# Evictions for both token blocks in one instruction, and a fourth pair by seven products in every other chunk of gate and up

## Chip, cores and metric

The kernel runs on one core of a Trainium2 chip. The metric is the device time of one execution in microseconds, as the median of several runs.

## What is computed

One layer of a streaming encoder on 256 tokens of width 2048, in f32. Two SwiGLU feed-forward blocks of width 5632 stand around a mixing stage (latent attention and gated linear attention) and a cross attention to 256 memory tokens. The change concerns the feed-forward blocks:

```python
def swiglu(h, w_gate, w_up, w_down):
    return (jax.nn.silu(h @ w_gate) * (h @ w_up)) @ w_down

x = x + 0.5 * swiglu(rmsnorm(x, ffn1_norm[l]), ffn1_w_gate[l], ffn1_w_up[l], ffn1_w_down[l])
...  # attention, gated linear attention, cross attention
x = x + 0.5 * swiglu(rmsnorm(x, ffn2_norm[l]), ffn2_w_gate[l], ffn2_w_up[l], ffn2_w_down[l])
```

## The kernel before

Tokens stand in two blocks (b = 0, 1) of 128. Every f32 product is made of three matmuls: each operand is split into a high part (rounded to the matmul's own type) and a low part, and high by high, high by low and low by high are added in PSUM. For weights, `parts` (L123) makes the high part with a cast on ScalarE (L128) and the low part with a subtraction on VectorE (L129), for every weight that is loaded.

A feed-forward block (`ffn`, L558) runs over eleven chunks of 512 columns of gate and up, in groups of four, four and three. After each group the down product of that group runs in two passes (n = 0, 2), each over 1024 columns. Each such stage is one call of `pair_gemm` (L223). It runs over units: one unit is a pair of 128-row slices of the contraction with 512 columns of gate and 512 of up (in the down pass, two blocks of 512 columns).

A unit is either plain or mixed. A plain unit is 2 slices by 2 token blocks by 2 column blocks by 3 parts, 24 matmuls. A mixed unit forms the same 2 by 2 by 2 block product by seven products in place of eight (a Strassen-Winograd scheme): 21 matmuls. It pays with sums: `mixed_parts` (L203) adds the raw weights into `wsum` in three VectorE instructions (L208, L213, L214) and splits seven forms in two goes, 1536 and 2048 columns wide, where a plain unit splits 2048 columns once. The activations of a mixed pair stand as seven sums too, made by `split_pair` (L367 to L380) through the scratch tile `f`, of which there is one.

In a gate and up chunk from the third on, the order of the pairs is 1, 0, 3, 2, 5, 4, 6, 7, and pairs 1, 3 and 5 are mixed (`ORDER8`, `MIXED8`, L52). Four of the seven products are summed over the mixed pairs in four PSUM banks of their own (`extra`), and `middle` (L297) combines them into four tiles after the last mixed unit, with one copy on ScalarE and four additions on VectorE. The other products and the plain ones go into four accumulators `acc`, one bank for each token block and column block.

After the last unit the chunk is evicted (L580 to L586): for each token block one subtraction, one Silu on ScalarE, one addition, and one product that also applies the factor of the row norm, 512 columns each. The result is transposed and split a stage later, by pieces in `self.pending` that `pair_gemm` takes up at its steps (L244), which stand after the last mixed unit, or at the end (L293).

Buffers: four for the split weights (`wspl`; a mixed unit takes two, a plain one one), three for raw weights, one for `wsum`. The gemms of the mixing stage (`gemm`, L132) use the same `acc` banks and evict them block by block. Loads of weights are issued by SyncE. The order on each engine's queue is drawn up when the program is built, from the order of the text and from what is ready.

## Time and profile before

| | us |
|---|---|
| median of 3 runs | 1876.89 |
| lowest, highest | 1876.79, 1877.93 |
| the profiled execution | 1876.87 |
| its span, first to last instruction | 1875.1 |
| TensorE (PE) busy | 1856.3 |
| VectorE (DVE) busy | 1556.9 |
| ScalarE (ACT) busy | 1016.0 |
| GpSimd (POOL) busy | 63.5 |

The granted clock of TensorE is 1.0 of full speed throughout. The first FFN runs from about 10 to 718 us, the mixing stage and the cross attention to about 1171, the second FFN to 1871. Recorded matmuls overlap, so their cost is read from start to start. A row of the timeline gives the start in us, the length in us, the engine, the line, the operation, what it writes and reads with shapes, and in brackets the idle time of the engine before it with what ended it.

### The profile page before, as it was taken

What the parts mean: (1) busy time and instruction counts of PE and PEld (TensorE: products, weight loads), DVE (VectorE), ACT (ScalarE), POOL (GpSimd) and SP (SyncE); (2) the same over time, 40 slices, a digit from 0 to 9 for tenths busy, and PEclk for the clock granted to TensorE, in tenths of its full rate; (3) what the DMA queues carried; (4) which work ended last, traced back from release to release, by engine and by line L of the source; (5) the groups of instructions that cost most, each with busy time, mean ns of one, the idle gap of its engine ahead of it and who ended that gap; (6) DMA issues with size and microseconds to landing.
All of it is one profiled execution on the core that took longest, in us unless ns stands there. A gap on an engine that the chain in (4) does not pass through costs nothing.

```text
span 1875.1 us, 21806 instructions
## 1 busy us (share of the span) xinstructions
PE 1856.3 (99%) x8418; PEld 1525.4 (81%) x8418; DVE 1556.9 (83%) x1691; ACT 1016.0 (54%) x1088; POOL 63.5 (3%) x114
## 2 busy tenths in 40 slices
PE   7999999999999999999999999999999999999999
PEld 6788888888888888788778888788888888888887
DVE  7999999889999996555565655999998899999897
ACT  6555454555445554665555665655544555445552
POOL 1000000000000100120100020000000000000000
PEclk9999999999999999999999999999999999999999
DMA  7566566655665545544435554656556665556653
GB/s 247 182 224 202 180 205 214 198 196 201 205 207 192 203 176 181 169 159 146 133 129 210 179 179 135 202 180 218 206 199 207 202 202 187 195 202 205 200 201 135
DMA packets 148072, 356.01 MB, mean 190 GB/s; under 512 B 11018, under 2 KB 11120, under 8 KB 147968
## 3 DMA queue, kind: packets, MB, share of 16 engines
q1 hardware_dynamic: 147360, 354.07, 56.4%
q8 instruction: 66, 1.08, 0.2%
q0 software_dynamic: 608, 0.55, 0.2%
q14 instruction: 38, 0.31, 0.0%
HBM read 352.48 MB, written 2.10 MB: 189 GB/s over the span
## 4 chain that ended last, share of the span: by engine, by line
PE 95%; ACT 2%; DVE 1%; issue 1%; DMA 0%; POOL 0%; SPq 0%; ACTq 0%
PE acc L241 57%; PE acc L142 19%; PE bank L241 14%; PE bank L350 2%; ACT wh L128 1%; ACT junk L384 1%; DVE wl L129 1%; PE bank L950 0%; PE bank L805 0%; PE bank L786 0%; DMA raw<-in_ffn_w_up_dram 0%; PE bank L949 0%; PE bank L1004 0%; PE bank L1013 0%; ACT hth L359 0%
## 5 line engine op out<-in xcount | busy, mean ns | idle before, releaser
L129 DVE TENSOR_TENSOR wl<-raw,wh 128x2048 fp32r<-128x2048 f32 (+4 forms) x405 | 716.6, 1771 | 177.0 <-ACT wh L128 175.8
L128 ACT CAST wh<-raw 128x2048 fp32r<-128x2048 f32 (+4 forms) x405 | 601.7, 1494 | 380.4 <-PE acc L241 146.9
L241 PE MATMUL acc<-wh,hth 128*128 128x512 f32 x1078 | 418.6, 393 | 5.3 <-ACT wh L128 3.6
L241 PE MATMUL acc<-wl,hth 128*128 128x512 f32 x1078 | 418.3, 390 | 1.4 <-DVE wl L129 1.4
L241 PE MATMUL acc<-wh,htl 128*128 128x512 f32 x1078 | 362.8, 390 | 0.0
L128 ACT CAST wh<-wsum 128x2048 fp32r<-128x2048 f32 x98 | 187.6, 1914 | 282.4 <-DVE wsum L214 223.5
L129 DVE TENSOR_TENSOR wl<-wsum,wh 128x2048 fp32r<-128x2048 f32 x98 | 224.5, 2291 | 38.0 <-ACT wh L128 37.9
L241 PEld LDWEIGHTS acc<-wh,hth 128*128 128x128 f32 x1078 | 202.8, 188 | 47.5 <-ACT wh L128 4.3
L241 PEld LDWEIGHTS acc<-wl,hth 128*128 128x128 f32 x1078 | 202.7, 188 | 43.5 <-DVE wl L129 2.4
L241 PEld LDWEIGHTS acc<-wh,htl 128*128 128x128 f32 x1078 | 202.7, 188 | 42.7
L241 PE MATMUL acc<-wh,actph 128*128 128x512 f32 x448 | 175.9, 393 | 0.0
L241 PE MATMUL acc<-wl,actph 128*128 128x512 f32 x448 | 174.4, 389 | 0.0
L241 PE MATMUL acc<-wh,actpl 128*128 128x512 f32 x448 | 145.6, 389 | 0.0
L208 DVE TENSOR_TENSOR wsum<-raw 128x1024 f32<-128x1024 f32 x98 | 119.5, 1220 | 3.6 <-DMA raw<-in_ffn_w_down_dram 1.5
L142 PE MATMUL acc<-wh,hth 128*128 128x512 f32 (+1 forms) x288 | 113.2, 395 | 0.0
L142 PE MATMUL acc<-wl,hth 128*128 128x512 f32 (+1 forms) x288 | 109.9, 383 | 0.0
L241 PE MATMUL bank<-wl,hth 128*128 128x512 f32 x264 | 103.6, 392 | 1.4 <-DVE wl L129 1.4
L241 PE MATMUL bank<-wh,htl 128*128 128x512 f32 x264 | 102.8, 389 | 0.0
L241 PE MATMUL bank<-wh,hth 128*128 128x512 f32 x264 | 98.6, 390 | 0.0
L241 PEld LDWEIGHTS acc<-wh,actpl 128*128 128x128 f32 x448 | 84.0, 188 | 17.9
L241 PEld LDWEIGHTS acc<-wh,actph 128*128 128x128 f32 x448 | 84.1, 188 | 17.0
L241 PEld LDWEIGHTS acc<-wl,actph 128*128 128x128 f32 x448 | 84.2, 188 | 16.9
(280 smaller groups left out, 2395.7 us busy)
## 6 DMA issues: line engine op xcount, KB each, us to landing
raw<-in_ffn_w_down_dram SPq DMA_DIRECT2D x88, 1024.0 KB, 5.0
raw<-in_ffn_w_gate_dram SPq DMA_DIRECT2D x175, 512.0 KB, 3.8
raw<-in_ffn_w_up_dram SPq DMA_DIRECT2D x175, 512.0 KB, 4.7
raw<-in_w_in_dram SPq DMA_DIRECT2D x24, 1024.0 KB, 5.1
raw<-in_w_out_dram SPq DMA_DIRECT2D x16, 1024.0 KB, 5.1
raw<-in_w_in_dram SPq DMA_DIRECT2D x8, 832.0 KB, 4.5
raw<-in_mem_w_k_dram SPq DMA_DIRECT2D x4, 1024.0 KB, 5.1
raw<-in_mem_w_q_dram SPq DMA_DIRECT2D x4, 1024.0 KB, 5.1
```

The lines of the kernel that those rows point to most:

```text
L128: self.last_act = nc.scalar.copy(out=wh, in_=src)
L129: self.last_dve = nc.vector.tensor_tensor(out=wl, in0=src, in1=wh.bitcast(F32), op=ALU.subtract)
L142: self.last_pe = nc.tensor.matmul(out=out[b][c][:, :w], lhsT=high, rhs=part[:, o:o + w], start=start, stop=stop)
L208: nc.vector.tensor_tensor(out=t[:, :2 * CW].rearrange("p (j n) -> p j n", j=2), in0=raw[:, CW:3 * CW].rearrange("p (j n) -> p j n", j=2), ...
L241: self.last_pe = nc.tensor.matmul(out=bank, lhsT=high, rhs=part, start=key not in seen, stop=stop)
L350: nc.tensor.transpose(out=t[:, i * P:(i + 1) * P], in_=src(b, k), identity=self.ident)
L384: self.nc.scalar.activation(out=junk[:, :width], in_=src, func=AF.Square, accum_out=out)
```

## The change

Accumulators become tiles of two banks, one for each column block, that hold both token blocks side by side, in `pair_gemm` and in `gemm`. With them the eviction of a gate and up chunk is one subtraction and one addition of 1024 columns, and one product of 1024 columns. The factor of the row norm is no longer applied by that product but by a second ScalarE pass after each Silu. In the down passes the additions into `xs` also take both token blocks at once, except for the last column block of the whole FFN.

Chunks 3, 5, 7 and 9 of gate and up take pair 4 as a fourth mixed pair and run in the order 1, 0, 3, 2, 5, 6, 4, 7. Since pair 4 is plain in the other chunks, its normalised input has a kind of its own, "both", with eight 128-column slots, of which four serve as the plain form. To make room in SBUF, the mask and `g_out` move from the constants into the work pool of the mixing stage (and their memsets and load to its head), the work tile `t` has five buffers in place of six, and the scratch of GpSimd's DMAs is halved.

```diff
+MIXED_ODD, ORDER_ODD = (1, 3, 4, 5), (1, 0, 3, 2, 5, 6, 4, 7)
+KINDS = {1: "mixed", 3: "mixed", 4: "both", 5: "mixed"}
...
-        self.acc = pool("acc", 4, space=bass.MemoryType.PSUM)
+        self.acc = pool("acc", 2, space=bass.MemoryType.PSUM)
...
+    def accumulators(self, n):
+        accs = [self.acc.tile([P, NB * CW], F32, name="acc") for _ in range(n)]
+        return [[acc[:, b * CW:(b + 1) * CW] for acc in accs] for b in range(NB)] + [accs]
...
-        out = [[self.acc.tile([P, CW], F32, name="acc") for _ in chunks] for _ in range(NB)]
+        out = self.accumulators(len(chunks))
...
+    PLAIN = {
+        "plain": {(0, 0): 0, (0, 1): 1, (1, 0): 2, (1, 1): 3},
+        "both": {(0, 0): 2, (0, 1): 7, (1, 0): 3, (1, 1): 1},
+    }
...
-        out = [[self.acc.tile([P, CW], F32, name="acc") for _ in range(2)] for _ in range(NB)]
+        out = self.accumulators(2)
...
-        mixed = [i for i, (p, _) in enumerate(units) if xs[p][0]]
+        mixed = [i for i, (p, _) in enumerate(units) if p in mixed]
...
-            x = lambda t, k, b: t[:, (2 * k + b) * P:(2 * k + b + 1) * P]
+            x = lambda t, k, b: t[:, self.PLAIN[kind][k, b] * P:(self.PLAIN[kind][k, b] + 1) * P]
...
-        p1, u3 = (self.sums.tile([P, CW], F32, name="su", bufs=4) for _ in range(2))
-        u4, v = (self.sums.tile([P, CW], F32, name="sg", bufs=2) for _ in range(2))
+        up, gate = (self.sums.tile([P, NB * CW], F32, name=name, bufs=n) for name, n in (("su", 2), ("sg", 1)))
+        p1, u3 = up[:, :CW], up[:, CW:]
+        u4, v = gate[:, :CW], gate[:, CW:]
...
-        nc.vector.tensor_tensor(out=s5, in0=a22, in1=a21, op=ALU.subtract)
+        nc.vector.tensor_tensor(
+            out=blocks(4), in0=blocks(1), in1=a21.unsqueeze(1).broadcast_to([P, 2, P]), op=ALU.subtract
+        )
         nc.vector.scalar_tensor_tensor(out=s6, in0=s5, scalar=-1.0, in1=a11, op0=ALU.mult, op1=ALU.subtract)
         nc.vector.tensor_tensor(out=s3, in0=s6, in1=a12, op=ALU.add)
-        nc.vector.tensor_tensor(out=a21, in0=a11, in1=a21, op=ALU.subtract)
...
+        if kind == "both":
+            at = slice(7 * P, 8 * P)
+            nc.scalar.activation(out=th[:, at], in_=t[:, :P], func=AF.Copy, scale=gain(0))
+            nc.vector.scalar_tensor_tensor(
+                out=tl[:, at], in0=t[:, :P], scalar=gain(0), in1=th[:, at].bitcast(F32), op0=ALU.mult, op1=ALU.subtract
+            )
...
-                        ht, [(wg, c * CW), (wu, c * CW)], 0,
-                        ORDER8 if c > 1 else ORDER_NEXT if c else ORDER_LOAD if ahead else ORDER_TURN,
+                        ht, MIXED_ODD if c % 2 and c > 1 else MIXED8, [(wg, c * CW), (wu, c * CW)], 0,
+                        ORDER_ODD if c > 1 and c % 2 else ORDER8 if c > 1 else ORDER_NEXT if c else ORDER_LOAD if ahead else ORDER_TURN,
...
-                    for b in range(NB):
-                        tt(out=sg[b], in0=out[b][0], in1=sg[b], op=ALU.subtract)
-                        nc.scalar.activation(out=sg[b], in_=sg[b], func=AF.Silu, scale=rstd()[:, b:b + 1])
-                    for b in range(NB):
-                        tt(out=a[b], in0=out[b][1], in1=a[b], op=ALU.add)
-                    for b in range(NB):
-                        stt(out=a[b], in0=a[b], scalar=rstd()[:, b:b + 1], in1=sg[b], op0=ALU.mult, op1=ALU.mult)
+                    tt(out=sg, in0=out[NB][0], in1=sg, op=ALU.subtract)
+                    for b, g in enumerate(halves(sg)):
+                        nc.scalar.activation(out=g, in_=g, func=AF.Silu, scale=rstd()[:, b:b + 1])
+                        nc.scalar.activation(out=g, in_=g, func=AF.Copy, scale=rstd()[:, b:b + 1])
+                    tt(out=a, in0=out[NB][1], in1=a, op=ALU.add)
+                    tt(out=a, in0=a, in1=sg, op=ALU.mult)
...
+                        up, gate = self.middle(extra)
+                        for c, t, f in ((1, up, 0.5), (0, gate, -0.5)):
+                            stt(out=xc[c], in0=both(t), scalar=f, in1=xc[c], op0=ALU.mult, op1=ALU.add)
...
+            self.mask = self.work.tile([P, 2 * P], F32, name="mask", bufs=1)
+            nc.gpsimd.memset(self.mask, 0.0)
+            nc.gpsimd.memset(self.mask[0:64, P + 64:2 * P], NEG)
+            self.g_out = self.work.tile([P, GV], F32, name="g_out", bufs=1)
+            nc.gpsimd.dma_start(out=self.g_out, in_=io["gla_out_norm"][0:1, :].broadcast_to([P, GV]))
...
-            zq = self.work.tile([P, CW], F32, name="t", bufs=6)
+            zq = self.work.tile([P, CW], F32, name="t", bufs=5)
...
-    nc = bacc.Bacc("TRN2", target_bir_lowering=False, num_devices=1, dynamic_dma_scratch_size=4096)
+    nc = bacc.Bacc("TRN2", target_bir_lowering=False, num_devices=1, dynamic_dma_scratch_size=2048)
```

## Rows read from the trace of the kernel before

**Rows 1.** The page, part 1: busy time, share of the span, instructions of each engine.

```profile
PE 1856.3 (99%) x8418; PEld 1525.4 (81%) x8418; DVE 1556.9 (83%) x1691; ACT 1016.0 (54%) x1088; POOL 63.5 (3%) x114
```

**Rows 2.** Timeline of chunk 3, first FFN: first matmuls of three successive units.

```profile
156.85 0.39 PE L241 MATMUL bank<-wh,hth 128*128 128x512 f32 x1
...
161.61 0.39 PE L241 MATMUL acc<-wh,hth 128*128 128x512 f32 x1
...
167.05 0.39 PE L241 MATMUL bank<-wh,hth 128*128 128x512 f32 x1
```

**Rows 3.** Busy time by stretch, chunks 1, 9, 10: length, then each engine (instructions).

```profile
61.45:104.21 42.76, 42.76 (x191) 34.98 (x192) 41.78 (x40) 25.33 (x20) 0.00 (x0) 1.00 0.59 190
...
567.19:609.62 42.43, 42.43 (x192) 35.14 (x191) 38.11 (x36) 23.83 (x18) 0.00 (x0) 1.00 0.61 199
609.62:652.06 42.44, 42.44 (x193) 35.13 (x191) 38.87 (x43) 22.56 (x16) 4.92 (x10) 1.00 0.59 199
```

**Rows 4.** Timeline of DVE from chunk 9 into chunk 10.

```profile
577.19 1.22 DVE L208 TENSOR_TENSOR wsum<-raw 128x1024 f32<-128x1024 f32 x1
...
579.78 1.75 DVE L129 TENSOR_TENSOR wl<-raw,wh 128x1536 fp32r<-128x1536 f32 x1
582.98 2.29 DVE L129 TENSOR_TENSOR wl<-wsum,wh 128x2048 fp32r<-128x2048 f32 x1 [1.45 <-ACT wh L128]
585.19 2.29 DVE L129 TENSOR_TENSOR wl<-raw,wh 128x2048 fp32r<-128x2048 f32 x1
...
603.00 2.28 DVE L129 TENSOR_TENSOR wl<-wsum,wh 128x2048 fp32r<-128x2048 f32 x1
...
609.91 1.28 DVE L584 TENSOR_TENSOR su<-acc,su 128x512 f32<-128x512 f32 x2
611.11 1.41 DVE L586 SCALAR_TENSOR_TENSOR su<-su,sm,sg 128x512 f32<-128x512 f32 x2
612.43 0.69 DVE L213 TENSOR_TENSOR wsum<-wsum,raw 128x512 f32<-128x512 f32 x1
```

**Rows 5.** Timeline of PE at the start of chunk 10: first extra, first accumulator.

```profile
609.62 0.39 PE L241 MATMUL bank<-wh,hth 128*128 128x512 f32 x1
...
612.35 0.39 PE L241 MATMUL acc<-wh,hth 128*128 128x512 f32 x1
```

**Rows 6.** Timeline of PE in the fourth unit of chunk 1: first and last matmul.

```profile
78.22 0.39 PE L241 MATMUL bank<-wh,hth 128*128 128x512 f32 x1
...
82.75 0.39 PE L241 MATMUL bank<-wh,htl 128*128 128x512 f32 x1
```

**Rows 7.** Timeline of DVE for that unit: its second low part.

```profile
78.98 2.29 DVE L129 TENSOR_TENSOR wl<-wsum,wh 128x2048 fp32r<-128x2048 f32 x1 [0.37 <-ACT wh L128]
```

**Rows 8.** Groups by line and form: count, busy us and mean ns, idle before.

```profile
L362 DVE SCALAR_TENSOR_TENSOR htl<-bank,gains,hth 128x256 fp32r<-128x256 f32 x52 | 23.8, 479 | 11.9 <-ACT hth L359 11.5
...
L380 DVE TENSOR_TENSOR htl<-f,hth 128x896 fp32r<-128x896 f32 x6 | 6.5, 1086 | 0.3 <-ACT hth L379 0.2
...
L375 DVE TENSOR_TENSOR f<-f 128x128 f32<-128x128 f32 x22 | 6.3, 284 | 0.6 <-ACT f L373 0.6
```

**Rows 9.** Timeline of PE where chunk 1 of the first FFN begins.

```profile
61.45 0.47 PE L241 MATMUL acc<-wh,hth 128*128 128x512 f32 x1 [1.67 <-DVE sg L581]
```

**Rows 10.** Timeline of DVE in chunk 0: end of one mixed split.

```profile
29.52 1.09 DVE L380 TENSOR_TENSOR htl<-f,hth 128x896 fp32r<-128x896 f32 x1 [0.25 <-ACT hth L379]
```

**Rows 11.** Timeline of ACT in chunk 0: beginning of the same split.

```profile
25.52 0.82 ACT L373 ACTIVATE f<-bank,gains 128x256 f32<-128x256 f32 x2
```

**Rows 12.** Timeline of PE where the second gemm of the mixing stage begins.

```profile
756.80 0.39 PE L142 MATMUL acc<-wh,hth 128*128 128x512 f32 x1
...
757.26 0.40 PE L142 MATMUL acc<-wh,hth 128*128 128x512 f32 x1
```

**Rows 13.** Timeline of DVE there: eviction of the second block.

```profile
757.00 0.51 DVE L699 COPY t<-acc 128x336 f32<-128x336 f32 x1 [1.08 <-PE acc L142]
```

**Rows 14.** Timeline of POOL at the end of the first FFN: the b_gate load.

```profile
705.78 0.59 POOL L679 DMA_DIRECT2D b_gate<-in_gla_b_gate_dram  x1 [49.03 <-DVE htl L362]
```

More of the change, by code (lines that the diff above doesn't have):

```diff
@@ L221, in mixed_parts, with pair_gemm @@
         return forms
-    def pair_gemm(self, xs, cols, k0, order, middle, ahead=None):
+    def pair_gemm(self, xs, mixed, cols, k0, order, middle, ahead=None):
         nc = self.nc
-        out = [[self.acc.tile([P, CW], F32, name="acc") for _ in range(2)] for _ in range(NB)]
+        out = self.accumulators(2)
         if ahead:
@@ L251, in pair_gemm @@
             last = u == len(units) - 1
-            is_mixed, xh, xl = xs[p]
+            is_mixed = u in mixed
+            kind, xh, xl = xs[p]
             with ExitStack() as first:
@@ L307, in middle @@
         add(u4, extra["p5"], u4)
-        return p1, u4, u3, v
+        return up, gate
     def later(self):
@@ L345, in split_pair @@
         nc = self.nc
-        mixed, th, tl = dst
+        kind, th, tl = dst
+        mixed = kind != "plain"
         t = self.bank()
@@ L384, in sum_sq, with new_ht @@
         self.nc.scalar.activation(out=junk[:, :width], in_=src, func=AF.Square, accum_out=out)
-    def new_ht(self, mixed=()):
-        pairs = []
+    def new_ht(self, kinds={}):
+        pairs, width = [], {"plain": 4 * P, "mixed": 7 * P, "both": 8 * P}
         for p in range(KD // 2):
-            width = (7 if p in MIXED8 else 4) * P
-            tiles = [self.keep.tile([P, width], F32R, name=f"ht{h}{p}") for h in "hl"]
-            pairs.append((p in mixed, *(t if p in mixed else t[:, :4 * P] for t in tiles)))
+            tiles = [self.keep.tile([P, width[KINDS.get(p, "plain")]], F32R, name=f"ht{h}{p}") for h in "hl"]
+            kind = kinds.get(p, "plain")
+            pairs.append((kind, *(t[:, :width[kind]] for t in tiles)))
         return pairs
@@ L477, in setup_mix @@
         bc = lambda ap, n: ap.broadcast_to([P, n])
-        self.g_out = const.tile([P, GV], F32, name="g_out")
-        nc.gpsimd.dma_start(out=self.g_out, in_=bc(io["gla_out_norm"][0:1, :], GV))
         freq = room[:, 0:32]
@@ L667, in mix_and_cross @@
             with left("mem") as mem:
-                mt = [(False, *(mem.tile([P, 4 * P], F32R, name=f"mt{h}{p}") for h in "hl")) for p in range(KD // 2)]
+                mt = [("plain", *(mem.tile([P, 4 * P], F32R, name=f"mt{h}{p}") for h in "hl")) for p in range(KD // 2)]
                 mss = self.sm([P, NB, NCH])
@@ L763, in gla_qk @@
         for b in range(NB):
-            gq = self.work.tile([P, CW], F32, name="t", bufs=6)
+            gq = self.work.tile([P, CW], F32, name="t", bufs=5)
             nc.scalar.activation(out=gq, in_=out[b][0], func=AF.Copy, scale=r1k[:, b:b + 1])
@@ L823, in gla_gate @@
             for c in range(2):
-                gate = self.work.tile([P, CW], F32, name="t", bufs=6)
+                gate = self.work.tile([P, CW], F32, name="t", bufs=5)
                 nc.scalar.activation(out=gate, in_=out[b][c], func=AF.Silu, scale=r1[:, b:b + 1])
@@ L1044, in raw @@
             for b in range(NB):
-                row = self.work.tile([P, CW], F32, name="t", bufs=6)
+                row = self.work.tile([P, CW], F32, name="t", bufs=5)
                 (nc.vector.tensor_copy if b else nc.scalar.copy)(out=row, in_=out[b][0])
@@ L1117, in run, with stage @@
         io = self.io
-        def stage(g, mixed=()):
+        def stage(g, kinds={}):
             ht, ss, r = [], self.sm([P, NB, NCH]), []
```

46 lines of the change are left out of this document (24 added, 22 removed).

## The prediction

> **What bounds the kernel now.** I read the busy table first, then the matmuls of one chunk in order of time, then the busy time by chunk, then VectorE (DVE) instruction by instruction, because the change puts work on DVE to take work off TensorE (PE). The reader is to see four things.
>
> PE is busy for 1856.3 of 1875.1 us [rows 1], and the matmuls of a chunk start at an even step. A mixed unit of 21 matmuls takes 161.61 - 156.85 = 4.76 us and a plain one of 24 takes 167.05 - 161.61 = 5.44 us, so one 512-column matmul costs 0.2267 us in both [rows 2]. PE sets the end.
>
> DVE is close behind. In chunk 9 of the first FFN it is busy 38.11 of 42.43 us, and in chunk 1, where it is pressed, 41.78 of 42.76 [rows 3]. So a pressed DVE still loses about 0.98 us in a chunk to dependences.
>
> In the settled chunks DVE runs ahead. The last part that the first unit of chunk 10 needs is finished at 603.00 + 2.28 = 605.28 [rows 4] and PE enters that unit at 609.62 [rows 5]: 4.3 us ahead. An idle time of it in chunk 9 (1.45 us before 582.98) ends with ScalarE's (ACT's) cast [rows 4], which itself has to wait for a buffer that PE gives back.
>
> Where DVE is late, PE's order can hide it. In a unit that begins at 78.22 [rows 6] the second half of the low parts lands at 78.98 + 2.29 = 81.27 [rows 7], 3.05 us after the unit has begun; yet its matmuls go on at 0.2265 us (78.22 to 82.75, twenty steps) [rows 6], because a product with another destination was put between.
>
> **The change part by part.** The sum is made against the profiled execution, 1876.87 us with a span of 1875.1; the median of the runs, 1876.89, is the same number.
>
> *Matmuls taken away.* Chunks 3, 5, 7 and 9 of each FFN turn pair 4 from plain (24 matmuls) into mixed (21). Eight pairs by 3 by 0.2267 us is **-5.44 us**, on the path, since PE sets the end. It can't be more; it is less by what follows.
>
> *DVE work added in those chunks.* A mixed unit costs DVE 2.59 us for the three sums (577.19 to 579.78), 1.67 for the first low part (1.75 recorded; starts come 0.08 before the recorded end) and 2.21 for the second (582.98 to 585.19), together 6.47; a plain one costs 2.21 [rows 4]. So +4.26 us. The evictions give some back. Two 512-column ones take 1.20 us (609.91 to 611.11) and the two products 1.32 (611.11 to 612.43) [rows 4]; with the gate's pair, costed like the up's, 3.72. In their place come three instructions of 1024 columns at 1.14 each, from the 1.22 recorded for that width less 0.08 [rows 4]: 3.42, a saving of 0.30. A merged eviction therefore saves little; DVE pays by the column. Chunk 9 then needs 38.11 + 4.26 - 0.30 = 42.07 and 0.98 of gaps, against PE's 42.43 - 0.68 = 41.75: DVE falls back by 1.3 us in an odd chunk. The even chunk after it, chunk 10, has 42.44 - 38.87 = 3.6 us of idle time to recover [rows 3].
>
> *The joint from an odd chunk to the next stage* (eight of them). The mixed pairs now end at the seventh unit and not at the fifth, so the four sums of the middle (4 by 0.60) and the two splits of the waiting activations (0.60, and 1.7 for a mixed one), 4.7 us by the same widths, come together with the evictions. DVE was 4.3 us ahead there [rows 4, 5]; 4.3 - 4.7 - 1.3 makes it about 1.7 us late in the next mixed units. PE hid 3.05 us of such lateness [rows 6, 7], so most of this should be hidden, with 1.3 us to spare. The four PSUM banks of the middle also have only one plain unit (5.44 us) to come free instead of three, and the second split's transposes come after the chunk. None of this is in the trace. Bounds: 0, by [rows 6]; 1.7 us a joint, if nothing is hidden. I take 0.15 a joint, near the row: **+1.2 us**. A gain is excluded, since the joint only gets more work.
>
> *ACT.* The factor of the row norm leaves DVE's product and becomes a second ACT pass over each 512-column half, and the new mixed units add two wide casts for one. ACT is busy 54% [rows 1] and has some 18 us idle in a chunk. The product waits longer for the second half, but what waits for the product is only the split a chunk later. If that cover went, it would cost the two added passes, about 1.4 us in a chunk; I take 0.
>
> *The first chunks.* Pair 4 of the normalised input gets the kind "both" in each FFN: its low parts cost two instructions of 0.40 spacing now (0.48 recorded), and then one of 896 columns (1.00), one of 256 (0.40) and three of 128 (0.20 each) [rows 8]: 2.0 for 0.8, or +1.2. The evictions of this chunk return 0.3. DVE is what PE waits for at the start, as at 61.45 [rows 9], so I put all of it on the path: 0.9 by 2, **+1.8 us**. Bounds: 0, if it falls into a wait for ACT or DMA; and 5.1 us in the first FFN, since the scratch tile f has one buffer, and a mixed split holds it from 25.52 [rows 11] to 29.52 + 1.09 [rows 10]. The row with the stop speaks for DVE's time, not for f, because pair 4 is needed only in the fourth unit.
>
> *Wider accumulators.* A tile now holds both token blocks of a chunk column and is given back when both are evicted. In FFN chunks that begin with a mixed pair this hides: the first product into it comes 2.73 us after the chunk's start (612.35 - 609.62) [rows 5], and the old evictions end at 611.19 [rows 4]. From chunk 0 to chunk 1 it does not: the first unit is plain, PE already waits 1.67 us there in the first FFN [rows 9], and one long instruction releases half an eviction later. I take **+0.4 us** for both FFNs (0 to 1.2).
>
> *Wider accumulators in the middle of the kernel.* The gemms between the FFNs use the same tiles, and some twelve of their joints evict block by block. One of them: the next gemm begins at 756.80 and its second column at 757.26 [rows 12]; the second block of the old column is copied from 757.00 to 757.51 [rows 13]. Before, that column only needed the first block. Now it waits 0.25 us, unless PE's order takes other products first, as in [rows 6]. Bounds 0 and 1.0 us a joint (a wider eviction with one instruction ahead of it). I take 0.05: **+0.6 us**.
>
> *Moves taken at nothing.* The mask's memsets and the load of g_out leave POOL's queue in the setup and go to the head of the mixing stage, ahead of the b_gate load, which is issued at 705.78 [rows 14] and used in the gemm that begins at 756.80 [rows 12]: some 50 us of cover. Five work buffers for six: never more than four are held but in the last head's overlap with the gates. Half the scratch of POOL's DMAs could delay the loads of the setup, a few us once; the trace shows no row for it, and I take 0. The merged additions into x save 0.1 us or so of DVE in the down stages, where it is not what PE waits for.
>
> Sum: -5.44 + 1.2 + 1.8 + 0.4 + 0.6 = -1.44, so 1876.87 - 1.44 = **1875.4 us**.
>
> **A rule weighed.** DVE's next instruction starts 0.08 us before the recorded end of the one before it (the pair at 609.91, recorded 1.28, is followed at 611.11) [rows 4]. The Trainium skill, VectorE: DVE Perf Modes, "The DRAIN you can't avoid", says that the next operation doesn't start until the pipeline is empty. If each of some 36 instructions of a chunk held DVE for its whole recorded time, an odd chunk would need 36 by 0.08 = 2.9 us more, and the joints would be 4.6 us late instead of 1.7, 1.55 beyond what PE's order hid: 8 by 1.55 in place of the 1.2 taken is 1886.6 us. The start-to-start times speak against it, and I give it 0.02.
>
> **The rivals.**
> *The whole saving arrives.* All joints are hidden and the split of pair 4 falls into waits: only 0.8 us or so is lost, 1872.2 us. For it: PE's even step under a late DVE [rows 6]. Against it: the stop at 61.45 [rows 9].
> *DVE becomes the bound at the joints* (slower). The order of the queues no longer hides the 1.7 us, each of the eight joints costs it, and 1875.4 - 1.2 + 13.6 = 1887.8 us. It decides from the point where a joint's lateness passes the 3.05 us that [rows 6, 7] show hidden; the step on which it hangs is the 4.7 us of work put in one place.
> *The accumulators' release* (slower). The twelve joints between the FFNs cost about 0.6 us each instead of 0.05: 1875.4 - 0.6 + 7.2 = 1882.0 us. For it: the time at 757.51 against 757.26. Against it: PE's free order.
> *The change doesn't do what it says*: the merged evictions leave DVE's time as it is, and the chunk lengths don't fall by 0.68 us because other waits fill them: about 1877.
>
> **How the numbers follow.** Forecast 0.50; whole saving 0.22; DVE bound at the joints 0.13; accumulators 0.11; the skill's rule 0.02; no effect 0.02. A measurement of this kernel can tell some 0.2%, or 3.75 us, from no change, so same means 1873.1 to 1880.6. Faster: 0.22. Slower: 0.13 + 0.11 + 0.02 = 0.26. Same: 0.52. The likeliest case has its own range of 1873 to 1880. The range runs from 1871.0 (the saving of 5.44 and some of DVE's at the start) to 1883.0 (the accumulators' case inside, the DVE case left out with the rule's, 0.15).
>
> **What would show it.** Odd chunks of 41.7 to 42 us on PE instead of 42.43, and even ones unchanged at 42.43, would show the saving and the joints right. A gap of PE in the first two units after an odd chunk, released by a low part or by a bank, shows the joint's price. The first chunk of each FFN longer by about 1 us shows pair 4; PE waits for the accumulators at the gemms' joints show that rival. DVE busy about 41.7 in an odd chunk shows the price of the mixed unit. The prediction is wrong if PE's step under a late DVE doesn't stay at 0.2267 us, or if a transfer or a bank that I count as covered turns up as PE's releaser.

## The result: 15.6 us slower

The changed kernel takes 1892.53 us (median of five runs, 1891.73 to 1894.05) against 1876.89 of the kernel before: a ratio of 1.0081, 95% interval 1.007 to 1.0093. The forecast was 1875.4 with a range of 1871.0 to 1883.0, so the time lies 9.5 us above the range. The profiled execution of after has a span of 1890.8 us, 15.7 more than that of before.

Part 1 of the page of after, which answers [rows 1]:

```profile
PE 1860.1 (98%) x8394; PEld 1523.2 (81%) x8394; DVE 1581.3 (84%) x1597; ACT 1049.5 (56%) x1144; POOL 55.5 (3%) x114
```

The 24 matmuls fewer are there (8418 to 8394), yet PE is busy 3.8 us longer (part of that is the granted clock, see the last section) and idle 12 us longer. What it waited for is the next view, the waits of PE in after: engine, tile and line that waited, what released it, then us in total, how often, the longest.

```profile
PE bank L254 <- DVE htl L403: 7.3, 1, 7.3
...
PE bank L1034 <- DVE s L1023: 1.4, 1, 1.4
PE acc L150 <- ACT t L855: 1.4, 1, 1.4
PE acc L254 <- DVE sg L599: 1.3, 2, 1.0
PE bank L1095 <- DVE t L1104: 1.2, 1, 1.2
PE bank L910 <- DVE rope L574: 1.1, 1, 1.1
PE acc L150 <- ACT v L903: 1.0, 1, 1.0
```

L254 is the matmul of the FFN stages, L150 that of the gemms between the FFNs; L910, L1034 and L1095 are the small work beside those gemms. Before had one such wait in the middle, 0.7 us on rope. So the places are the start of the first FFN (7.3 in one stop) and the middle (many of 1 to 1.4). The settled chunks answer [rows 3]; chunks 1, 9 and 10 of after (length, then busy time and instructions of PE, PEld, DVE, ACT, POOL, granted clock, DMA):

```profile
66.94:109.47 42.53, 42.53 (x192) 35.26 (x192) 41.34 (x34) 24.94 (x20) 0.00 (x0) 1.00 0.60 198
571.05:612.66 41.61, 41.61 (x189) 34.48 (x188) 37.65 (x31) 24.23 (x19) 0.00 (x0) 1.00 0.63 203
612.66:655.45 42.79, 42.79 (x194) 35.07 (x193) 41.69 (x43) 26.67 (x24) 4.90 (x10) 1.00 0.58 198
```

PE is without idle time here: the odd chunk fell from 42.43 to 41.61, the next rose from 42.44 to 42.79. That is a gain of 0.47 a pair of chunks, 3.8 us in eight, near the 4.24 (5.44 less 1.2) of the sum. The loss lies elsewhere.

The table has the length of each stretch, from the first product of a stage to that of the next, as the difference to before in us (the last stretch ends where the last product starts). *Moves* has the moved tiles and one thing more of the change, the split of a mixed pair, which makes two of its four 128-column sums in one instruction of 256 columns; all columns to its right and after have both. *Pair* adds the fourth pair without two-bank accumulators, *wide* the reverse, *middle* is the whole change with one-bank accumulators in the gemms; *best* is the run of the fourth pair in chunks 4, 6, 8 (and 10), with late sums. They are told below.

| stretch | before | after | moves | pair | wide | middle | best |
|---|---|---|---|---|---|---|---|
| up to the first product | 10.35 | -1.8 | -2.3 | -2.0 | -2.2 | -2.0 | -2.2 |
| first FFN, chunk 0 | 51.10 | +7.3 | +0.1 | +4.1 | +1.6 | +7.4 | +0.1 |
| first FFN, rest | 657.37 | -2.0 | 0.0 | +1.1 | +2.5 | -1.4 | -2.0 |
| middle (all gemms) | 453.34 | +10.7 | +0.4 | +0.3 | +10.7 | +0.4 | +0.3 |
| second FFN, chunk 0 | 44.73 | +2.6 | -1.2 | -1.2 | +2.1 | +0.3 | -1.2 |
| second FFN, rest | 653.63 | -1.8 | 0.0 | -2.7 | +2.2 | -1.7 | -2.5 |

### The profile page after: what moved, and what is told of

The parts are those of the page before. It is cut to its first block, busy times and chain, and to the rows that moved or that the text cites. A ratio compares the mean times of both kernels' runs of the same rounds, so it can differ in the third digit from the quotient of the medians.

```text
span 1890.8 us, 21665 instructions
## 1 busy us (share of the span) xinstructions
PE 1860.1 (98%) x8394; PEld 1523.2 (81%) x8394; DVE 1581.3 (84%) x1597; ACT 1049.5 (56%) x1144; POOL 55.5 (3%) x114
## 3 DMA queue, kind: packets, MB, share of 16 engines
q8 instruction: 66, 1.08, 0.2%
## 4 chain that ended last, share of the span: by engine, by line
PE 94%; ACT 2%; DVE 1%; issue 1%; DMA 1%; POOL 1%; SPq 0%; DVEq 0%; ACTq 0%
PE acc L254 56%; PE acc L150 18%; PE bank L254 15%; PE bank L366 2%; ACT wh L136 1%; ACT junk L409 1%; DMA raw<-in_ffn_w_up_dram 1%; PE bank L980 0%; PE bank L835 0%; PE bank L816 0%; PE bank L979 0%; PE bank L1034 0%; PE bank L1043 0%; DVE wl L137 0%; POOL sm L97 0%
## 5 line engine op out<-in xcount | busy, mean ns | idle before, releaser
L254 PE MATMUL acc<-wh,hth 128*128 128x512 f32 x1038 | 407.1, 394 | 3.9 <-ACT wh L136 2.6
L254 PE MATMUL acc<-wl,hth 128*128 128x512 f32 x1038 | 406.2, 392 | 0.8 <-DVE wl L137 0.7
L136 ACT CAST wh<-wsum 128x2048 fp32r<-128x2048 f32 x106 | 202.7, 1913 | 276.1 <-DVE wsum L227 226.4
L254 PE MATMUL acc<-wh,htl 128*128 128x512 f32 x1038 | 354.3, 391 | 0.4 <-DVE htl L378 0.4
L137 DVE TENSOR_TENSOR wl<-wsum,wh 128x2048 fp32r<-128x2048 f32 x106 | 242.8, 2291 | 44.0 <-ACT wh L136 43.9
L254 PEld LDWEIGHTS acc<-wh,hth 128*128 128x128 f32 x1038 | 195.8, 189 | 45.7 <-ACT wh L136 3.2
L254 PEld LDWEIGHTS acc<-wl,hth 128*128 128x128 f32 x1038 | 196.1, 189 | 42.0 <-DVE wl L137 2.2
L254 PEld LDWEIGHTS acc<-wh,htl 128*128 128x128 f32 x1038 | 195.6, 189 | 42.2 <-DVE htl L378 1.1
L254 PE MATMUL acc<-wh,actph 128*128 128x512 f32 x448 | 175.8, 393 | 0.0
L254 PE MATMUL acc<-wl,actph 128*128 128x512 f32 x448 | 174.3, 389 | 0.0
L254 PE MATMUL acc<-wh,actpl 128*128 128x512 f32 x448 | 145.8, 389 | 0.0
L221 DVE TENSOR_TENSOR wsum<-raw 128x1024 f32<-128x1024 f32 x106 | 129.2, 1219 | 1.5 <-DMA raw<-in_ffn_w_up_dram 0.9
L254 PE MATMUL bank<-wh,hth 128*128 128x512 f32 x296 | 112.5, 393 | 7.3 <-DVE htl L403 7.3
L254 PE MATMUL bank<-wl,hth 128*128 128x512 f32 x296 | 116.2, 392 | 0.0
L254 PE MATMUL bank<-wh,htl 128*128 128x512 f32 x296 | 115.6, 391 | 0.0
L150 PE MATMUL acc<-wh,hth 128*128 128x512 f32 (+1 forms) x288 | 113.8, 395 | 1.3 <-ACT v L903 1.0
L150 PE MATMUL acc<-wl,hth 128*128 128x512 f32 (+1 forms) x288 | 110.1, 383 | 0.0
L254 PEld LDWEIGHTS acc<-wh,actpl 128*128 128x128 f32 x448 | 84.1, 188 | 17.7
L254 PEld LDWEIGHTS acc<-wl,actph 128*128 128x128 f32 x448 | 84.2, 188 | 17.0
L254 PEld LDWEIGHTS acc<-wh,actph 128*128 128x128 f32 x448 | 84.1, 188 | 17.0
```

The lines of the kernel that those rows point to most:

```text
L136: self.last_act = nc.scalar.copy(out=wh, in_=src)
L137: self.last_dve = nc.vector.tensor_tensor(out=wl, in0=src, in1=wh.bitcast(F32), op=ALU.subtract)
L150: self.last_pe = nc.tensor.matmul(out=out[b][c][:, :w], lhsT=high, rhs=part[:, o:o + w], start=start, stop=stop)
L221: nc.vector.tensor_tensor(out=t[:, :2 * CW].rearrange("p (j n) -> p j n", j=2), in0=raw[:, CW:3 * CW].rearrange("p (j n) -> p j n", j=2), ...
L254: self.last_pe = nc.tensor.matmul(out=bank, lhsT=high, rhs=part, start=key not in seen, stop=stop)
```

## Experiments

### Which half of the change, and which gemms

One-bank accumulators in the gemms alone, the rest of the change kept (the mixing stage opens a pool of four banks, each FFN one of two tiles of two banks):

```diff
-        out = self.accumulators(len(chunks))
+        out = [[self.acc.tile([P, CW], F32, name="acc") for _ in chunks] for _ in range(NB)]
...
+            self.acc_pool(weights, 4)
```

> The changed kernel, but the gemms between the two FFNs have one-bank accumulators again (four of 512 columns, each token block with its own), while gate, up and down keep the two-bank ones. Theory A (the release of the two-bank accumulators makes the 10.8 us that the stretch from the end of the first FFN to the start of the second lost): that stretch returns to within 1 us of the kernel before, and the time to about 1892.5 - 10.8 = 1881.7 us. Theory B (the five work buffers in place of six, or the mask and g_out set up late, make it): the stretch stays 10 us longer, about 1892.5. The first 60 us are unchanged in both: TensorE stops for about 7.3 us at 25.6.

Measured: 1881.18 us, ratio 1.0019 (1.0009 to 1.0028). The middle returns to +0.4, and 2.3 of the 2.6 us at the start of the second FFN go with it; those are time at a lower granted clock (last section). Theory A holds; the five work buffers and the late mask and g_out cost the middle 0.4 us at most.

The change without the fourth pair:

```diff
-MIXED_ODD, ORDER_ODD = (1, 3, 4, 5), (1, 0, 3, 2, 5, 6, 4, 7)
-KINDS = {1: "mixed", 3: "mixed", 4: "both", 5: "mixed"}
+KINDS = {1: "mixed", 3: "mixed", 5: "mixed"}
...
```

> The changed kernel without the fourth mixed pair: no chunk has it and pair 4 is split plainly, everything else of the change stays (two-bank accumulators, merged evictions, moved tiles, five work buffers). Theory A: the 10.8 us of the middle stay, the stop at the start (5.5 us in the first FFN, 2.5 in the second) goes, and the saving of the chunks (3.8 us) goes too: 1876.9 + 10.8 = 1887.7, with 0.4 more at most for the joint of the first chunks. Theory C (the middle is late only because the fourth pair leaves late work of the first FFN to it): about 1877.

Measured: 1894.62 us, ratio 1.0089 (1.0074 to 1.0104), 6.9 us above what Theory A gave. The middle is the +10.7 of after, so Theory C falls. What I had not counted is the FFNs: with the wide evictions and without the fourth pair they are 1.6 + 2.5 + 2.1 + 2.2 us longer than before. Part of it stands in PE's waits of this run, at the down stages, for activations of the last chunk that come late:

```profile
PE acc L253 <- DVE actpl L370: 3.3, 5, 0.9
```

The fourth pair alone (with the moves and the split):

```diff
-        self.acc = pool("acc", 2, space=bass.MemoryType.PSUM)
+        self.acc = pool("acc", 4, space=bass.MemoryType.PSUM)
...
-                    tt(out=sg, in0=out[NB][0], in1=sg, op=ALU.subtract)
...
+                        tt(out=sg[b], in0=out[b][0], in1=sg[b], op=ALU.subtract)
```

> The other half alone: the fourth mixed pair, the kind both and the moved tiles with five work buffers, but the accumulators and evictions of the kernel before (one bank each, block by block). Theory A: the middle is as before, so 1876.9 + 5.5 + 2.5 - 3.8 = 1881.1 us. Theory B: the moves are still in it, so about 1892. The stop of 7.3 us at 25.6 stays in both.

Measured: 1875.72 us, ratio 0.9987 (0.9977 to 0.9996): a small gain where 1881 was expected. The middle is clean again. Two-bank tiles in the FFNs are thus worth 5.5 us of loss (1881.18 - 1875.72). One thing is new here: stage dn8.0 of the first FFN, the first down pass after chunks 8 to 10, is 4.1 us longer.

Whether the instruction or the tile costs those 5.5 us: the run with one-bank gemms, where gate and up evict their shared tiles in 512-column instructions as before.

```diff
-                    tt(out=sg, in0=out[NB][0], in1=sg, op=ALU.subtract)
...
+                        tt(out=s_[b], in0=out[b][0], in1=s_[b], op=ALU.subtract)
+                        nc.scalar.activation(out=s_[b], in_=s_[b], func=AF.Silu, scale=rstd()[:, b:b + 1])
```

> The run with one-bank accumulators in the middle (1881.2 us), where gate and up now evict their two-bank tiles in 512-column instructions, token block by token block, with the row factor in the product, as the kernel before; the tiles are still shared by both blocks. The runs with and without the FFNs' two-bank tiles and merged evictions stand 5.5 us apart (1881.2 and 1875.7): 0.2 us in each of eight joints, 3.4 in the first chunk of the first FFN, 1.5 in that of the second. Theory K (the instruction of 1024 columns and the chain through a second ScalarE pass cost it): nearly all of it returns, about 1876.5. Theory L (the shared tile costs it: what is given back later, or read only when both blocks are written): it stays, 1881.

Measured: 1880.88 us, ratio 1.0015 (1.0006 to 1.0024). Nothing returns, Theory L: it is not the width of the eviction, but what the two blocks share. The stage after a chunk with the fourth pair is 0.30 us longer with halves, 0.34 with wide instructions and 0.13 with one-bank tiles. This run keeps the merged additions into x and the sums' tiles in SBUF, which both blocks share too; that the PSUM tile is what costs was shown for the gemms (below), not for the FFNs.

### How a shared tile costs time in a gemm

DVE and PE where the second gemm begins; first after, which answers [rows 12, 13] (L729 copies out of the accumulators, L736 is a transpose beside the gemm):

```profile
760.42 0.32 PE L150 MATMUL acc<-wh,htl 128*128 128x336 f32 x1
...
760.78 0.92 DVE L729 COPY t<-acc 128x336 f32<-128x336 f32 x2 [2.32 <-PE acc L150]
...
761.34 0.28 PE L736 MATMUL bank<-ident,t 128*16 128x128 f32 x1 [0.60 <-DVE t L729]
761.85 0.47 PE L150 MATMUL acc<-wh,hth 128*128 128x512 f32 x1 [0.23 <-DVE t L729]
```

then the run with one-bank gemms (L735 is the same copy, L154 the same matmul):

```profile
758.55 0.51 DVE L735 COPY t<-acc 128x336 f32<-128x336 f32 x1
...
760.50 0.32 PE L154 MATMUL acc<-wh,htl 128*128 128x336 f32 x1
760.66 0.39 PE L154 MATMUL acc<-wh,hth 128*128 128x512 f32 x1
...
760.86 0.51 DVE L735 COPY t<-acc 128x336 f32<-128x336 f32 x1 [1.08 <-PE acc L154]
```

With one-bank tiles the copy of the first token block runs at 758.55, while PE is still at the second block, and the next gemm follows in 0.16 us. With the shared tile both copies stand after the last product (760.42 + 0.32 = 760.74, copies from 760.78), although the first block was done over 2 us earlier. The next gemm starts 1.43 us after that product. The transposes that the queue puts ahead need the same copy and wait for it too, which is why the waits of the middle bear names like t and rope and not only acc.

If it is that, the order of the products should return it where a gemm has two column blocks:

```diff
-            order = [(c,) for c in range(len(chunks))] if last else [tuple(range(len(chunks)))]
-            turns = [(b, cs, j) for b in range(NB) for cs in order for j in range(nk)]
-            if not last:
+            edge = last or not i
+            order = [(c,) for c in range(len(chunks))] if edge else [tuple(range(len(chunks)))]
+            turns = [(b, cs, j) for cs in order for b in range(NB) for j in range(nk)]
+            if not edge:
```

> The changed kernel with its two-bank accumulators, but the gemms between the FFNs go through their first and last slab of weights by column block and not by token block: all products into the first accumulator tile (both token blocks), then all into the second. Theory F (in the middle the eviction of a two-bank tile starts only after the last product into it, so the first token block's eviction no longer runs under the second one's products): with this order the first tile is complete half a slab before the end again and the next gemm starts on it; the joints of gemms with two column blocks (GQ, k0, GV, k1, ZR, wo0, 8.3 us in sum in the change) fall to under 2 us together, while those of the gemms with one column block, whose only tile can't be complete early (mk to mo0, 3.8 us), stay; the time is about 1892.5 - 6.5 = 1886. Theory G (a two-bank tile costs at any order, by its release or by two engines in its banks at once): the joints stay, about 1892.

Measured: 1887.62 us, ratio 1.0051 (1.0035 to 1.0066), 4.9 below after. The stage that ends at the joint into GV, 1.99 us longer in after than before, is 0.10 longer here; at the joint into ZR 2.38 became 0.72. In sum (net of what next stages give back) the gemms with two column blocks fell from 6.4 to 3.4 us, those with one stayed (3.9 and 4.1). The last gemm, with two column blocks again, gives 1.2 more, and chunk 0 of the second FFN 1.1. Theory F holds in kind; it returned half and not three quarters. PE at that joint, after and then this run:

```profile
828.85 0.27 PE L910 MATMUL bank<-ident,rope 128*128 128x128 f32 x1
830.14 0.50 PE L150 MATMUL acc<-wh,hth 128*128 128x512 f32 x1 [1.02 <-ACT v L903]
```

```profile
828.29 0.27 PE L911 MATMUL bank<-ident,q 128*128 128x128 f32 x1
828.39 0.50 PE L150 MATMUL acc<-wh,hth 128*128 128x512 f32 x1
```

### The start of the first FFN

In after PE stands still from 25.90 to 33.16; the rows of ACT, DVE and PE answer [rows 9 to 11] (L389 copies pair 4's transposes into f, L403 makes the low part of its eighth slot from the bank of the transposes, L399 is the last use of f by the split before, L366 are transposes):

```profile
24.87 1.03 PE L366 MATMUL bank<-ident,xs 128*128 128x128 f32 x8
...
27.52 1.08 DVE L399 TENSOR_TENSOR htl<-f,hth 128x896 fp32r<-128x896 f32 x1
...
28.20 1.89 ACT L136 CAST wh<-wsum 128x2048 fp32r<-128x2048 f32 x1
29.99 0.84 ACT L389 ACTIVATE f<-bank,gains 128x256 f32<-128x256 f32 x2
...
32.67 0.34 DVE L403 SCALAR_TENSOR_TENSOR htl<-bank,gains,hth 128x128 fp32r<-128x128 f32 x1
...
33.16 0.77 PE L254 MATMUL bank<-wh,hth 128*128 128x512 f32 x1 [7.26 <-DVE htl L403]
```

What waits is the first product of a mixed unit, for one of its four banks, which pair 4's split still holds. f, with one buffer, is free of the split before at 27.52 + 1.08 = 28.60, and ACT, which makes a cast until 30.09, copies pair 4 into it only from 29.99. The first run takes the eighth slot from f, so that the bank is free sooner:

```diff
+        if kind == "both":
+            at = slice(7 * P, 8 * P)
+            nc.scalar.copy(out=th[:, at], in_=a21)
+            nc.vector.tensor_tensor(out=tl[:, at], in0=a21, in1=th[:, at].bitcast(F32), op=ALU.subtract)
...
-            nc.scalar.activation(out=th[:, at], in_=t[:, :P], func=AF.Copy, scale=gain(0))
```

> The changed kernel, but the eighth slot of pair 4 (high and low part) is made from the scratch tile f, ahead of the sums that overwrite it, and no longer from the PSUM bank of the transposes, so that this bank comes free when f has been copied, as for the other mixed pairs. Theory D (the stop at 25.6 us is the wait of the first mixed unit for that bank, which the eighth slot's low part gives back last): the stop shortens from 7.3 to the time at which f is copied, about 30.8, so by about 2.2 us, and the time falls by 2 to 3 us, to about 1890; the stop then ends with the copy into f. Theory E (the stop is DVE's load and f's single buffer alone, the bank is no part of it): the stop keeps its 7 us and the time stays at 1892.5.

Measured: 1893.66 us, ratio 1.0081 (1.0066 to 1.0096), no gain. The stop itself is shorter by 2.3 us, as Theory D said, and ends with the copy into f, but other waits follow and chunk 1 begins at 66.94 as in after:

```profile
PE bank L254 <- ACT f L389: 5.0, 1, 5.0
...
PE acc L254 <- DVE wl L137: 1.6, 1, 1.6
...
PE bank L254 <- DVE htl L378: 1.0, 1, 1.0
```

So the bank sets where PE stops, and the work of the fourth mixed split sets when chunk 0 ends. To take that work away, on one-bank accumulators: pair 4 is split plainly, and its sums are made in chunk 2 from its own high and low parts.

```diff
+    def sum_pair(self, dst):
...
+        tt(out=f[:, :4 * P], in0=th[:, :4 * P].bitcast(F32), in1=tl[:, :4 * P].bitcast(F32), op=ALU.add)
...
+                    if c == 1:
+                        self.pending.append(lambda: self.sum_pair(ht[4]))
```

> The fourth mixed pair with the accumulators and evictions of the kernel before (as in the run with that half alone, 1875.7 us), but pair 4 is split plainly at the start, and its four sums are made in the third chunk, from its high and low parts, by five DVE instructions and one ScalarE cast. Theory D (what the start lost, 4.1 us in the length of the first chunk, is the mixed form of pair 4, by f and by the bank): the stop of TensorE at 25 us is gone and the first chunk is as long as before (51.1 us); time about 1875.7 - 4 = 1872 us. Theory H (the start is later by the moved set-up of the constants): the first chunk stays 4 us longer and the time at 1875.7. The stretch dn8.0 of the first FFN (set-up of the mixing stage, 4.1 us longer with the fourth pair alone) is unchanged in both.

Measured: 1873.79 us, ratio 0.9978 (0.9969 to 0.9987). The stop is gone and chunk 0 is 0.8 us longer in place of 4.1 (it begins 2.3 us sooner). Theory D. But the stage after chunk 3 is now 1.03 and 1.30 us longer in the two FFNs, so 1.9 us are left of the expected 4.

### DVE's reserve

Without the fourth pair in chunk 9 of the first FFN:

```diff
+        odd = (3, 5, 7) if ahead else (3, 5, 7, 9)
```

> The same with late sums, and chunk 9 of the first FFN without the fourth pair (chunks 3, 5, 7 there, 3, 5, 7, 9 in the second). Theory I (the 4.1 us of the stretch dn8.0 come from DVE, which has the fourth pair's work of chunk 9 still to make up when the set-up of the mixing stage is put on it): the stretch is as before, at the price of one saving of 0.67, so 3.4 us below the kernel with late sums, about 1868.5. Theory J (an accident of the order, not DVE's load): the stretch stays longer and the time is 0.7 above the kernel with late sums.

Measured: 1872.00 us, ratio 0.9968 (0.9956 to 0.9981). dn8.0 is as long as before (0.01 us more), Theory I: DVE still owed work when the set-up of the mixing stage was put on it. The gain is 1.8 us and not 3.4, since that stage was only 2.4 us longer in the run with late sums; the rest of the 4.1 with the fourth pair alone was the granted clock (last section). The load is not the whole cause: after and the run with one-bank gemms have the fourth pair in chunk 9 too, and dn8.0 is not longer there (+0.01 and +0.03 us). In those two the set-up's work on DVE begins 3.5 us into the stage, in the two runs that lose 1.0. So its place in the queue counts as well, and Theory J is not excluded.

The same seven chunks, moved away from chunk 3:

```diff
-        odd = (3, 5, 7) if ahead else (3, 5, 7, 9)
+        odd = (4, 6, 8) if ahead else (4, 6, 8, 10)
```

> Late sums as before, with the fourth pair in chunks 4, 6, 8 of the first FFN and 4, 6, 8, 10 of the second, so seven as in the run with 3, 5, 7 and 3, 5, 7, 9 (1872.0 us), but never in the chunk right after the one that makes the late sums. In that run the stage after chunk 3 was 1.03 and 1.29 us longer, against 0.13 after the other chunks. Theory O (DVE has not made up the late sums and the start when chunk 3 begins): these 2.1 us go, 1869.9 us. Theory P (the stage after the first chunk with the fourth pair is longer whichever it is): 1872.

Measured: 1869.74 us, ratio 0.9957 (0.9944 to 0.9969), where 1869.9 was expected. Theory O. This run is faster than the kernel before by 0.43%, and than the change by 1.2%.

And in every chunk of gate and up from 4 on, but 9 and 10 of the first FFN:

```diff
+        odd = (4, 5, 6, 7, 8) if ahead else (4, 5, 6, 7, 8, 9, 10)
```

> The fourth pair in every chunk from the fifth on: 4 to 8 of the first FFN, 4 to 10 of the second, twelve in all. By DVE's need as the prediction worked it out (42.07 us and 0.98 of gaps, so 43.05 in such a chunk against 41.75 of TensorE), DVE falls back 1.3 us in each and has no chunk to recover except the down stages. Theory Q (that sum is right, and DVE's lead of 4.3 us is used up by the second chunk in a row): the third and fourth in a row are longer, 42 to 43 us, and the time is not under that of seven chunks, 1870 to 1874. Theory R (DVE's need is overstated, since TensorE hides late parts): each chunk brings its 0.67, twelve of them 3.4 us more than seven: about 1867.

Measured: 1884.33 us, ratio 1.0033 (1.002 to 1.0047), 10 us above the 1870 to 1874 that were expected. Busy time in chunks 4 to 7 of the first FFN, columns as above:

```profile
271.81:312.61 40.80, 40.80 (x181) 33.78 (x180) 38.16 (x33) 21.91 (x14) 0.00 (x0) 1.00 0.61 206
312.61:354.31 41.70, 41.70 (x190) 34.40 (x188) 40.30 (x36) 23.90 (x19) 0.00 (x0) 1.00 0.60 201
354.31:397.69 43.38, 42.65 (x192) 34.26 (x190) 41.61 (x39) 21.87 (x17) 0.00 (x0) 1.00 0.50 171
397.69:442.71 45.02, 43.03 (x191) 34.24 (x190) 43.66 (x40) 26.56 (x21) 0.00 (x0) 1.00 0.54 187
```

Two chunks in a row are short, the third and fourth are not, with DVE pressed (43.66 of 45.02). Theory Q in kind; the price in the pressed chunk is some 2 us above the 43.05 of the sum.

### The moved set-up

The moves and the split, with nothing else of the change:

```diff
-        nc.gpsimd.dma_start(out=self.g_out, in_=bc(io["gla_out_norm"][0:1, :], GV))
...
+            self.g_out = self.work.tile([P, GV], F32, name="g_out", bufs=1)
+            nc.gpsimd.dma_start(out=self.g_out, in_=io["gla_out_norm"][0:1, :].broadcast_to([P, GV]))
```

> The kernel before with the moved tiles alone (mask and g_out set up at the head of the mixing stage, five work buffers, half the scratch of GpSimd's DMAs), no fourth pair, accumulators and evictions as before. In every run with the moves TensorE's first product starts about 2 us earlier. Theory M (the moves give a gain of their own: two things fewer in the set-up): 1876.9 - 2 = 1875 us, the middle unchanged. Theory N (the 2 us are lost again in the first chunk, which waits for the loads of x and weights anyway): 1877.

Measured: 1873.97 us, ratio 0.9976 (0.9968 to 0.9985), a gain of 3.9 us where the prediction had the moves at nothing. 2.3 us come ahead of the first product, 1.2 in chunk 0 of the second FFN. Since the split is in it, this run does not show the moves by themselves.

The load of g_out moved by its line alone:

```diff
-        nc.gpsimd.dma_start(out=self.g_out, in_=bc(io["gla_out_norm"][0:1, :], GV))
...
+            nc.gpsimd.dma_start(out=self.g_out, in_=io["gla_out_norm"][0:1, :].broadcast_to([P, GV]))
```

> The kernel before with one line moved: the load of g_out (128 KB, one row broadcast to 128 partitions) is issued at the head of the mixing stage and not in the set-up. Its tile, the mask, the six work buffers and the scratch stay as they were. Theory S (that load takes the DMA engines from x and the first weights in the first 10 us; the trace of the kernel before has them move as little as 89 GB/s around 6 us, and without it 253 to 307 there): the first product starts 2 us earlier, as with all the moves, and the time is 1876.9 - 2.2 = 1874.7, or 1874 if the 1.2 us of the second FFN's first chunk belong to it too. Theory T (the scratch, the mask's memsets or the five buffers): 1877.

Measured: 1877.96 us, ratio 0.9999 (0.999 to 1.0008). It told nothing, since the load did not move: its tile was free, so it was put into POOL's queue at the old place (row one). The first cast of weights waits as before (row two):

```profile
1.85 0.78 POOL L634 DMA_DIRECT2D g_out<-in_gla_out_norm_dram  x1
...
9.05 1.04 ACT L128 CAST wh<-raw 128x1024 fp32r<-128x1024 f32 x1 [1.56 <-DMA raw<-in_ffn_w_up_dram]
```

With the tile in a pool that opens after the first FFN:

```diff
-        self.g_out = const.tile([P, GV], F32, name="g_out")
...
+            self.g_out = self.work.tile([P, GV], F32, name="g_out", bufs=1)
```

> The kernel before, with g_out's tile in the work pool of the mixing stage and its load issued there (the pool opens only after the first FFN, so the load can't be drawn ahead, as it was in the last run); five work buffers for t, since the tile needs the room. Mask and scratch as before. Theory S (the load of g_out in the set-up delays the first weights): the first product starts at about 8.1 us in place of 10.35, and the time is 1874 to 1875. Theory T (the halved scratch, or the mask's memsets, make the earlier start): the first product starts at 10.2 again, and 1877.

Measured: 1876.06 us, ratio 0.999 (0.998 to 0.9999). The first product starts at 8.19, Theory S, and the cast waits for no load:

```profile
7.11 1.04 ACT L128 CAST wh<-raw 128x1024 fp32r<-128x1024 f32 x1
```

Of the 2.2 us, 0.75 are lost in chunk 0 and 0.73 in dn8.0; the span is 0.5 us below that of before, the median 1.9 below the 1877.96 that before measured beside it. So this load explains the earlier start, and at most half of the 3.9. What the rest is (mask, scratch, the split, or the queue order that comes with them) stays open. For the 1.2 us in the second FFN the split is the nearest candidate, though it was not run by itself: chunk 0 there, where DVE splits pair after pair, is 44.73 us before, 44.76 and 44.73 in the last two runs, which have the old split, and 43.51 to 43.55 in the six runs with the new split, all the moves and one-bank tiles everywhere.

## Why the prediction was wrong, point by point

- **Matmuls right, joints near.** -5.44 + 1.2 was forecast for the eight pairs of chunks, -3.8 measured. Of the 0.68 that three matmuls are worth, the chunk and the stage after it keep 0.47 with shared tiles, so a joint costs 0.21, 1.7 us in eight. With one-bank tiles they keep 0.65 (-0.78, then +0.13), so the joint itself costs 0.03. The 0.15 taken lies between the two; that the total came near is in part luck, since the 0.2 belongs to the shared tiles and not to the work that was counted.
- **DVE's need: right in kind.** The odd chunk's surplus did not show where it was said (DVE busy 41.7 in chunk 9). It shows a chunk later: 37.65 in chunk 9, 41.69 in chunk 10, over both 2.4 us more than before where the sum has 3.7 (4.26 less two evictions' 0.30). PE ran on, and every second chunk made it up; without that chunk DVE becomes the bound, as the rival said. The rival itself (1887.8) did not happen.
- **Wider accumulators in the middle: the step that failed most.** 0.05 us a joint was taken, 0.6 in sum, with 1.0 a joint as the upper bound; 10.7 were measured, 0.9 a joint over the twelve, 2.4 in the two worst. [rows 13] show the second block's copy, and I read from it when the column comes free. I took the first block's copy as staying where it was; that is the step that failed. It had stood under the second block's products, and a shared tile moves it behind them. The rival *accumulators' release* had the place right and the price (0.6) too low. "PE's free order" was no argument: what is put ahead waits for the same copies.
- **Wider accumulators in the FFNs: too low.** 0.4 us for the first chunks, nothing for the rest; 5.5 by the medians of the two runs with and without them, 4.0 by their profiled executions (1878.8 and 1874.8). It is a net figure: with the shared tiles chunk 0 is 3.4 us longer in the first FFN and 1.5 in the second, and the eight joints 0.2 each, while the 4.1 us of dn8.0 are gone.
- **First chunks: 1.8 us forecast.** Chunk 0 of the first FFN became 7.2 us longer than with the moves alone. "Pair 4 is needed only in the fourth unit" looked at the unit that reads pair 4. The one that stopped was a mixed unit, for a bank that pair 4's split held through f. The bound of 5.1 us was there in the text, and I put it aside. About 4 of the 7 come with the fourth pair (the run with it alone), 1.5 with the wide tiles alone; why both together cost 1.7 more was not isolated. In the second FFN the fourth pair costs chunk 0 nothing (-1.2 with it and with the moves alone), where 0.9 was taken.
- **Moves at nothing: wrong in sign,** 3.9 us of gain together with the split, at least the 2.2 ahead of the first product from the load of g_out. I asked what the moved load costs at its new place, and never what it had cost at its old one.
- **The skill's rule:** DVE in after still starts the next instruction ahead of the recorded end, here 65.58 + 1.22 = 66.80 against 66.71. So that rival did not happen, and the loss has other causes. The prediction took only half of the paragraph: the Trainium skill (VectorE: DVE Perf Modes, "The DRAIN you can't avoid") adds that a next operation which is not held starts earlier. The trace agrees with that, by 0.09 us.

```profile
65.58 1.22 DVE L599 TENSOR_TENSOR sg<-acc,sg 128x1024 f32<-128x1024 f32 x1
66.71 1.21 DVE L603 TENSOR_TENSOR su<-acc,su 128x1024 f32<-128x1024 f32 x1
```

In the sum: moves -3.9, fourth pair with its start +1.8, shared tiles in the FFNs +5.5, in the gemms with what they bring on at the second FFN +11.3 (1892.53 - 1881.18): 14.7. Each term is the difference of two runs that follow each other in this row, so they must add up to 1892.53 less the 1877.88 that before measured beside the moves, and the sum is no proof of the parts; the 15.6 is taken from the 1876.89 of another measurement of before. In another order the parts would be of other sizes: without the fourth pair, the wide tiles lose 2.5 and 2.2 us in the chunks after the first ones, with it less.

## To carry to other kernels

Before an accumulator is made to hold two blocks, look where the first block's eviction lies: if it runs under the second block's products, the merge takes that cover away, and merging saves little: DVE took 1.13 us from start to start for 1024 columns (65.58 to 66.71) and 1.20 for two of 512 [rows 4]. A wait that is sized from one row needs the row of the instruction that came before it too. A step moved in the text is moved only if something (its tile, its pool) keeps it from being drawn back, and what it leaves behind at its old place is part of the sum.

## Not expected of the hardware

After the stop, TensorE came back at the lower of its two levels. Busy time and granted clock (the column after POOL) around the stop in after:

```profile
26.00:30.00 4.00, 0.00 (x0) 0.00 (x0) 3.39 (x4) 4.00 (x9) 0.00 (x0) 1.00 0.50 150
30.00:33.00 3.00, 0.00 (x0) 0.00 (x0) 2.88 (x4) 3.00 (x9) 0.00 (x0) 0.53 0.69 266
33.00:37.00 4.00, 3.84 (x9) 2.68 (x10) 3.96 (x7) 2.67 (x4) 0.00 (x0) 0.50 0.01 4
37.00:42.00 5.00, 5.00 (x23) 4.14 (x22) 3.94 (x9) 1.78 (x3) 1.79 (x2) 1.00 0.64 211
```

and in the run with the fourth pair alone, where PE stopped for 4.4 us up to 29.36:

```profile
24.00:29.00 5.00, 0.95 (x9) 0.71 (x7) 4.91 (x8) 4.67 (x11) 0.00 (x0) 1.00 0.53 192
29.00:36.00 7.00, 6.54 (x15) 4.65 (x16) 6.89 (x10) 6.43 (x13) 0.00 (x0) 0.51 0.45 149
```

At 0.5 of 2.4 GHz, so 1.2, products of 512 columns start every 0.43 us in place of 0.227:

```profile
33.80 0.63 PE L248 MATMUL bank<-wh,hth 128*128 128x512 f32 x1
34.23 0.63 PE L248 MATMUL bank<-wl,hth 128*128 128x512 f32 x1
34.66 0.63 PE L248 MATMUL bank<-wh,htl 128*128 128x512 f32 x1
```

In the second case some 15 products ran so: 15 by 0.2 is 3 us beside the 4.4 of the stop. Chunk 0 is only 4.1 us longer there, since waits that it had before fall into the stop. In the best kernel, which has no such stop, the granted clock from 20 to 40 us is 1.00. A stop can thus cost more than the idle time, and the prediction's bound of 5.1 us had left that out.

The same happened in two more places, without a stop of that length. One is the start of the second FFN. Here is its chunk 0 in after, a part of it, and the whole chunk in the run with one-bank gemms:

```profile
1186.39:1233.67 47.28, 45.86 (x191) 37.18 (x192) 44.80 (x48) 29.95 (x35) 1.77 (x2) 0.93 0.61 200
1187.00:1194.00 7.00, 5.91 (x18) 4.64 (x18) 6.95 (x10) 7.00 (x14) 0.00 (x0) 0.52 0.38 117
```

```profile
1176.58:1221.60 45.02, 43.50 (x192) 34.97 (x192) 44.60 (x48) 30.60 (x33) 1.77 (x2) 1.00 0.65 211
```

PE's idle time is the same in both (1.42 and 1.52 us); the whole difference of 2.3 us is busy time at the lower clock. So these 2.3 us of the loss are no wait, though they go with the gemms' shared tiles. Why the clock fell in the one run and not in the other is not shown. The other place is dn8.0 with the fourth pair alone:

```profile
677.70:681.10 3.40, 3.40 (x10) 2.66 (x9) 3.33 (x5) 0.06 (x1) 0.00 (x0) 0.50 0.93 355
```

PE is busy 34.31 us in that stage, and 32.70 in the run with late sums, where the clock stays at 1.00: 1.6 of the 4.1 us.
